# Layer 0 of a two-layer trunk: the kv latent normed ahead of its split, key copies and rotary digit products on ScalarE, and 8 instead of 16 diagonal convolution products on TensorE

## The chip, the core and the metric

The kernel is one program on one core of a Trainium2 chip. Five engines work beside each other, each through its own list of instructions in order: TensorE (PE; its weight loads are listed apart as PEld), VectorE (DVE), ScalarE (ACT), GpSimd (POOL) and SyncE (SP), which only issues transfers. The metric is device time in microseconds (us) of one execution; less is better.

## The reference

The input is 512 tokens of 1024 channels, in float32. Layer 0, which alone is touched, is a mixer in two branches followed by a gated MLP:

```python
proj = h @ w_in                          # h = rmsnorm(x)
# branch A: 512 channels
u = a * jax.nn.sigmoid(g)
u = causal_dwconv(u, conv_w, conv_b)     # 31 taps per channel
u = jax.nn.silu(layernorm(u, conv_ln_g, conv_ln_b))
# branch B: latent attention, 8 heads, causal, blocks of 128 queries
q  = rmsnorm(cq, q_norm_g) @ w_uq        # cq: 384 columns of proj
kv = rmsnorm(ckv, kv_norm_g) @ w_ukv     # ckv: 256 columns of proj
kn, v = kv[..., :64], kv[..., 64:]
# qr, kr are turned by cos, sin of position * inv_freq
o = mla_attention(qn, qr, kn, kr, v)
x = x + concat([u, o]) @ w_out
```

Layer 1 has a pooling mixer instead, and the same MLP. A last rmsnorm ends the trunk.

## The kernel before

Channels lie on the 128 partitions and the 512 tokens on the free axis, so that one projection of 128 columns is a sum of products 128x128 by 128x512 in a bank of PSUM. For float32 precision every operand is split in a high and a low part (`split`, lines 96 to 99: ACT copies the high part, DVE subtracts it from the source), and `mm3` (107 to 110) makes three products of the parts. Each weight tile of 128x1024 comes from memory through SP, and is split by the same two lines; three weight tiles can be held in parts at a time, so ACT can start on the next one only when TensorE has done with the oldest.

The order of each engine's instructions is set by a scheduler when the program is built, from the order of the code, buffers and dependencies; once built, it is fixed, and an engine whose next instruction waits does nothing else.

Layer 0 goes as follows.

- Start: x and the first weights arrive, xg = x times gain is split, and four banks are summed (356, 357). Meanwhile `rotary` (317 to 347) makes the tables of cosine and sine: an angle in two parts times five digits gives ten tiles `rope` of 128x64 (324, 325), which `fold` (313) reduces. The row sums of x*x go through small products on TensorE (`rstd`, 239), a reciprocal square root on DVE (205 to 212) and products with a diagonal on TensorE (`spread`, 260, 261), and ACT copies the result (265): a tile `rows` that holds the scale of each token on all partitions.
- Projections: `project` (364) makes one bank from 24 products. `latent` (448) makes three of cq and two of ckv: each is split from PSUM with its gain (102, 103), before its norm is known, and its squares are summed. After one more projection (kr) `rstd` gives the scales of q and kv together (465). Two pairs a and g of branch A follow.
- Attention (565 to 595): `keys_of` makes the keys of two heads and scales them on DVE by `rows_kv` (487), for which `spread` runs at the first call (483); the values are scaled by ACT (582). Each head has `scores` (product 511, DVE mask and maximum 514, ACT exponential 525, ACT scaling 532), `transposes` (546, ACT copies 548) and `values` (558).
- The convolution runs in the background. Channel tiles 0 to 2 are summed by DVE, one `tap` (400) for each of 30 shifts after an opening by ACT (383), in the PSUM tile `conv`. For tile 3 the first `PE_TAPS` = 16 shifts are products with a diagonal on TensorE (393; POOL makes the diagonal, 392), two in each of the eight heads, in the tile `aux`, and DVE does the other 15 there. `pump` (422) hands out these steps during the projections and heads; `pump(200, 200)` (595) hands out what is left behind the last head. `close` (415) copies the finished tile to `side`.
- End of the mixer: TensorE sums the attention half of the output projection (`half`), transposes the four `side` tiles (623), DVE takes mean and variance (625, 626), the reciprocal root and the scaling follow (634 to 637), TensorE transposes back (648), ACT applies silu (650), and the convolution half of the output projection follows (674 to 681), then the residual (663).

Of the kernel before, what the change touches and what calls it, by code (L numbers as in the profile page):

```python
# [8 lines left out]
F32 = mybir.dt.float32  # L9
F32R = mybir.dt.float32r  # L10
I32 = mybir.dt.int32
AF = mybir.ActivationFunctionType
ALU = mybir.AluOpType
# [11 lines left out]
SCALE = 1.0 / math.sqrt(96.0)  # L25
# [7 lines left out]
C_NE, C_CB, C_LG, C_LB, C_QG, C_KG, C_NO, C_PS, C_NF, C_FN = 0, 8, 12, 16, 20, 23, 25, 33, 41, 57  # L33
# [3 lines left out]
N_COL = C_FB + 2 * NF  # L37

WARM = 40
PE_TAPS = 16  # L40
PAD = 184
GLU, LAT, BLK, END = 3, 4, 2, 0

# [2 lines left out]
def kernel(  # L46
# [20 lines left out]
    act, dve, pool, pe = nc.scalar, nc.vector, nc.gpsimd, nc.tensor  # L67
# [21 lines left out]
    def temp():  # L89
        return p_t.tile([P, 2 + S], F32, tag="t", name=uid("t"))[:, :S]  # L90
# [5 lines left out]
    def split(dst, src):  # L96
        i = act.copy(dst[0], src)  # L97
        dve.tensor_tensor(dst[1], src, dst[0].bitcast(F32), op=ALU.subtract)  # L98
        return i
# [12 lines left out]
    def pair(t, lo=0, hi=S):  # L112
        if isinstance(t, tuple):
            return t[0][:, lo:hi], t[1][:, lo:hi]
        return t[:, 0, lo:hi], t[:, 1, lo:hi]
# [61 lines left out]
    spare, floor, q_scale = misc[:, 0:1], misc[:, 4:8], misc[:, 8:12]  # L177
# [3 lines left out]
    ps = bank()  # L181
# [7 lines left out]
    def c(i):  # L189
        return col[:, i : i + 1]  # L190
# [39 lines left out]
    def rstd(stats, blocks=range(4), floor=None, keep=None):  # L230

        ps = aux()
        nb = len(blocks)
        v = small(nb * len(stats))
        for k, st in enumerate(stats):
            for i, b in enumerate(blocks):
                at = 2 * (nb * k + i)
                for n, t in enumerate(st.parts):
                    pe.matmul(  # L239
                        ps[:, at : at + 2], t[:, b * P : (b + 1) * P], ones[:, 0:2],  # L240
                        start=n == 0, stop=n == len(st.parts) - 1,
                    )
            cols_of = ps[:, 2 * nb * k : 2 * nb * (k + 1) : 2]
            vk = v[:, nb * k : nb * (k + 1)]
            if floor is None:
                dve.tensor_scalar(vk, cols_of, 1.0 / st.n, EPS, op0=ALU.mult, op1=ALU.add)
            else:
                dve.scalar_tensor_tensor(
                    vk, cols_of, 1.0 / st.n, floor, op0=ALU.mult, op1=ALU.add
                )  # L250
        if keep is not None:
            dve.tensor_scalar(keep, v, EPS, None, op0=ALU.mult)
        return rsqrt(v, nb * len(stats))
# [10 lines left out]
    def spread(r, dst):  # L264
        act.copy(dst, spread_bank(r, 4))

    def rows_tile():
        return p_t.tile([P, S], F32, tag="rows", bufs=2, name=uid("rows"))
# [31 lines left out]
    ah = p_t.tile([P, 64], F32R, tag="rope_h", bufs=1, name="ah")  # L300
# [7 lines left out]
    ang, al, yt, yc, rr = (rt[:, i, :] for i in range(5))  # L308
# [8 lines left out]
    def rotary():  # L317
        dve.tensor_copy(yt, pos_i)
        dve.tensor_scalar(ang, yt, dig[:, 0:1], None, op0=ALU.mult)
        dve.tensor_copy(ah, ang)  # L320
        dve.tensor_tensor(al, ang, ah.bitcast(F32), op=ALU.subtract)
        for j in range(5):
            d = dig[:, 1 + j : 2 + j]
            dve.tensor_scalar(pr[:, 2 * j, :], ah.bitcast(F32), d, None, op0=ALU.mult)
            dve.tensor_scalar(pr[:, 2 * j + 1, :], al, d, None, op0=ALU.mult)
        fold(pr, rd, HUGE)
        fold(pr, rd, BIG)
        dve.tensor_reduce(yt, pr.rearrange("p j t -> p t j"), axis=AX.X, op=ALU.add)
        fold(yt, rr, BIG)
        dve.tensor_scalar(yc, yt, 0.25, None, op0=ALU.add)  # L330
        fold(yc, rr, BIG)
        for v in (yt, yc):
            dve.tensor_scalar(v, v, -TURN_LIMIT, TURN_LIMIT, op0=ALU.max, op1=ALU.min)
        for i, (v, s) in enumerate(((yc, 1.0), (yt, -1.0), (yt, 1.0))):
            act.activation(trig[:, i, :], v, AF.Sin, scale=s * 2.0 * math.pi)
        bounce = p_d.tile([64, S], F32, name="rope_rows")
        for g, i in enumerate((0, 0, 1, 2)):
            nc.sync.dma_start(
                bounce[g * 16 : (g + 1) * 16, :].rearrange("f (b t) -> (f b) t", b=8),
                trig[:, i, :],  # L340
            )
        pool.memset(ctab[0][0:64, :], 1.0)
        pool.memset(ctab[1][64:128, :], 1.0)
        nc.sync.dma_start(ctab[0][64:128, :], bounce)
        nc.sync.dma_start(ctab[1][0:64, :], bounce)
        nc.sync.dma_start(ktab[0:64, :], bounce)
        nc.sync.dma_start(ktab[64:128, :], bounce)
# [16 lines left out]
    def project():  # L364
        w = weights()
        ps = bank()
        for k in range(KD):
            mm3(ps, part(w, k), pair(xg[k]), k == 0, k == KD - 1)
        return ps
# [52 lines left out]
    def pump(nd, np_=0):  # L422
        for _ in range(min(np_, len(pe_work))):
            pe_work.pop(0)()
        for _ in range(min(nd, len(work))):
            work.pop(0)()
# [16 lines left out]
    def s4():  # L443
        return p_m.tile([P, 2, S], F32R, tag="s4", bufs=8, name=uid("s4"))
# [3 lines left out]
    def latent(n, gain, width):  # L448
        parts, stat = [], Squares(width, dve)
        for m in range(n):  # L450
            ps = project()
            parts.append(s4())
            split_scaled(pair(parts[m]), ps, c(gain + m))
            stat.add(ps)
            pump(LAT)
        return parts, stat

    cq, stat_q = latent(3, C_QG, 384)
    ckv, stat_kv = latent(2, C_KG, 256)

    ps = project()
    dve.tensor_tensor(ktab, ktab, rows0, op=ALU.mult)
    kt = temp()
    dve.tensor_tensor(kt, ps, ktab, op=ALU.mult)
    r = rstd([stat_q, stat_kv], floor=floor)
    r_q, r_kv = r[:, 0:4], r[:, 4:8]
    dve.tensor_scalar(q_scale, r_q, SCALE, None, op0=ALU.mult)
    for _ in range(2):
        ps_a = project()
        pump(GLU)  # L470
# [7 lines left out]
    def keys_of(hp):  # L478
        ps = bank()
        for k in range(2):  # L480
            mm3(ps, part(wk, k * 4 + hp), pair(ckv[k]), k == 0, k == 1)
        if hp == 0:
            spread(r_kv, rows_kv)
        ks = keys[hp % 2]
        for e in range(2):
            a, b = e * 64, e * 64 + 64
            dve.tensor_tensor(ks[a:b, e, :], ps[a:b, :], rows_kv[a:b, :], op=ALU.mult)

    qs, probs, pts, sums, att = {}, {}, {}, {}, []
    wq = [None]  # L490
# [71 lines left out]
        a = e * 64  # L562
        split(rows_of(att[hp], a, a + 64), ps[a : a + 64, :])

    rows_kv = rows_tile()
    queries(0)
    queries(1)
    ps = bank()
# [8 lines left out]
    for j in range(4):  # L577
        ps = bank()
        for k in range(2):
            mm3(ps, pair(ckv[k], j * P, (j + 1) * P), part(wv, k, S), k == 0, k == 1)  # L580
        v = p_a.tile([P, S], F32, tag="v", bufs=4, name=uid("v"))
        act.activation(v, ps, AF.Copy, scale=r_kv[:, j : j + 1])
        vals.append(v)
    for h in range(HEADS):
        scores(h)
# [415 lines left out]
```

## Time and profile before

| | us |
|---|---|
| median of 3 runs | 1013.87 |
| lowest, highest run | 1013.25, 1014.61 |
| the profiled execution's own time | 1013.5 |
| its span, first to last instruction | 1011.7 |
| TensorE busy | 994.0 (98%) |
| VectorE busy | 591.6 (58%) |
| ScalarE busy | 400.7 (40%) |
| GpSimd busy | 70.8 (7%) |

Busy times are those of the profiled execution, over its whole span. Layer 0's mixer takes the first 222 us or so of it; the remaining 790 us, in which the MLPs lie, are outside of the change. Times of day below count from the span's first instruction. A row of the profile gives a line of the kernel, the engine, the operation, what is written and what is read (numbers of buffers left out), and shapes. Consecutive instructions of an engine overlap, so a duration is a little longer than the step from one start to the next: a convolution tap on DVE lasts 0.74 to 0.75 us, and the next instruction starts 0.66 us after it if it doesn't need the tap's result.

### The profile page before, as it was taken

To read this page: it belongs to the slowest core of one execution; us is meant where nothing else is said; L and a number is where in the kernel's file an instruction comes from. 1 tells how busy PE (TensorE), PEld (TensorE's weight loads), DVE (VectorE), ACT (ScalarE), POOL (GpSimd) and SP (SyncE) were. 2 spreads that over 40 slices of the span, in tenths; PEclk is the share of its full clock that TensorE was granted. 3 is DMA by queue.
4 is the path that set the end of the run, shared out by engine and by line. 5 is a ranking of instruction groups with operands and counts; after the bars stand their busy time and mean duration, and the time that the engine had idled before them with its cause. 6 is when DMAs were issued, how large, how long until landed. Compare 5 with 4: busy or idle time off the path is not lost.

```text
span 1011.7 us, 11545 instructions
## 1 busy us (share of the span) xinstructions
PE 994.0 (98%) x4476; PEld 797.1 (79%) x4476; DVE 591.6 (58%) x915; ACT 400.7 (40%) x581; POOL 70.8 (7%) x107
## 2 busy tenths in 40 slices
PE   8999999999999999999999999999999999999996
PEld 6787676777888888888888889888888888888886
DVE  5889989856766565656332338485656555522223
ACT  6534687553433333333222236253333333332321
POOL 6000100012000000000001103100000000000101
PEclk9999999999999999999999999999999999999998
DMA  6422101113232323232222241322232223222212
GB/s 213 153 79 88 54 10 63 42 42 124 68 121 84 104 87 102 84 103 90 98 93 95 95 144 43 105 86 102 83 105 91 97 86 102 95 93 96 92 42 84
DMA packets 29478, 91.99 MB, mean 91 GB/s; under 512 B 4080, under 2 KB 6384, under 8 KB 29424
## 3 DMA queue, kind: packets, MB, share of 16 engines
q1 hardware_dynamic: 28880, 90.74, 27.3%
q8 instruction: 35, 0.57, 0.2%
q10 hardware_dynamic: 544, 0.52, 0.1%
q14 instruction: 19, 0.16, 0.0%
HBM read 89.02 MB, written 2.23 MB: 90 GB/s over the span
## 4 chain that ended last, share of the span: by engine, by line
PE 92%; DVE 4%; issue 1%; ACT 1%; DMA 0%; POOL 0%; SPq 0%; DVEq 0%
PE ps L108 28%; PE ps L110 28%; PE ps L109 28%; PE ps L558 2%; PE ps L511 1%; DVE lo L98 1%; PE aux L393 1%; PE ps L546 1%; PE aux L261 1%; PE aux L239 1%; DVE xgl L103 1%; DMA x<-in_xT_dram 0%; POOL sqr L226 0%; PE ps L869 0%; PE ps L870 0%
## 5 line engine op out<-in xcount | busy, mean ns | idle before, releaser
L108 PE MATMUL ps<-xgh,hi 128*128 128x512 f32 x816 | 324.0, 397 | 3.1 <-ACT hi L97 3.1
L97 ACT CAST hi<-raw 128x1024 fp32r<-128x1024 f32 (+2 forms) x166 | 170.0, 1026 | 394.2 <-PE ps L109 371.3
L110 PE MATMUL ps<-xgh,lo 128*128 128x512 f32 x816 | 323.3, 397 | 0.8 <-DVE lo L98 0.8
L109 PE MATMUL ps<-xgl,hi 128*128 128x512 f32 x816 | 323.4, 396 | 0.0
L98 DVE TENSOR_TENSOR lo<-raw,hi 128x1024 fp32r<-128x1024 f32 (+2 forms) x166 | 201.7, 1216 | 159.8 <-ACT hi L97 159.4
L108 PEld LDWEIGHTS ps<-xgh,hi 128*128 128x128 f32 x816 | 153.7, 188 | 40.2 <-ACT hi L97 3.7
L110 PEld LDWEIGHTS ps<-xgh,lo 128*128 128x128 f32 x816 | 153.8, 189 | 39.0 <-DVE lo L98 2.2
L109 PEld LDWEIGHTS ps<-xgl,hi 128*128 128x128 f32 x816 | 153.7, 188 | 36.6
L108 PE MATMUL ps<-gh,hi 128*128 128x512 f32 (+1 forms) x374 | 143.0, 382 | 0.0
L109 PE MATMUL ps<-gl,hi 128*128 128x512 f32 (+1 forms) x374 | 142.8, 382 | 0.0
L110 PE MATMUL ps<-gh,lo 128*128 128x512 f32 (+1 forms) x374 | 142.8, 382 | 0.0
L108 PEld LDWEIGHTS ps<-gh,hi 128*128 128x128 f32 x374 | 70.3, 188 | 15.0
L110 PEld LDWEIGHTS ps<-gh,lo 128*128 128x128 f32 x374 | 70.3, 188 | 15.0
L109 PEld LDWEIGHTS ps<-gl,hi 128*128 128x128 f32 x374 | 70.3, 188 | 15.0
L698 DVE TENSOR_TENSOR t<-ps,rows 128x512 f32<-128x512 f32 x44 | 30.4, 690 | 82.7 <-PE ps L110 82.7
L710 DVE TENSOR_TENSOR t<-ps,rows 128x512 f32<-128x512 f32 x44 | 30.4, 690 | 74.0 <-PE ps L110 74.0
L226 POOL TENSOR_TENSOR sqr<-sqr,sqr 128x512 f32<-128x512 f32 x33 | 50.5, 1529 | 322.2 <-ACT sqr L224 292.0
L400 DVE SCALAR_TENSOR_TENSOR conv<-u,col,conv 128x512 f32<-128x512 f32 x90 | 67.5, 750 | 1.6 <-ACT conv L383 0.7
L705 DVE SCALAR_TENSOR_TENSOR t<-t,col,t 128x512 f32<-128x512 f32 x88 | 65.6, 748 | 1.4
L708 ACT ACTIVATE t<-t 128x512 f32<-128x512 f32 x44 | 27.8, 632 | 74.2 <-DVE t L705 74.2
L103 DVE SCALAR_TENSOR_TENSOR xgl<-x,col,xgh 128x512 fp32r<-128x512 f32 x32 | 32.7, 1038 | 12.9 <-ACT xgh L102 12.9
L108 PE MATMUL ps<-s,hi 128*128 128x512 f32 x96 | 39.3, 421 | 0.0
(182 smaller groups left out, 813.6 us busy)
## 6 DMA issues: line engine op xcount, KB each, us to landing
raw<-in_w_up_dram SPq DMA_DIRECT2D x88, 512.0 KB, 3.3
raw<-in_w_down_dram SPq DMA_DIRECT2D x44, 512.0 KB, 3.3
raw<-in_w_in_dram SPq DMA_DIRECT2D x10, 512.0 KB, 3.3
raw<-in_w_out_dram SPq DMA_DIRECT2D x8, 512.0 KB, 3.3
x<-in_xT_dram SPq DMA_DIRECT2D x8, 256.0 KB, 4.7
raw<-in_w_in_dram SPq DMA_DIRECT2D x8, 256.0 KB, 4.0
raw<-in_w_uq_dram SPq DMA_DIRECT2D x4, 384.0 KB, 3.0
raw<-in_w_ukv_dram SPq DMA_DIRECT2D x2, 512.0 KB, 3.5
```

The costliest lines, as they stand in the source:

```text
L97: i = act.copy(dst[0], src)
L98: dve.tensor_tensor(dst[1], src, dst[0].bitcast(F32), op=ALU.subtract)
L103: dve.scalar_tensor_tensor(dst[1], src, scale, dst[0].bitcast(F32), op0=ALU.mult, op1=ALU.subtract)
L108: pe.matmul(ps, a[0], b[0], start=start, stop=False)
L109: pe.matmul(ps, a[0], b[1], start=False, stop=False)
L110: pe.matmul(ps, a[1], b[0], start=False, stop=stop)
L226: self.engine.tensor_tensor(self.parts[0], self.parts[0], t, op=ALU.add)
L400: i = dve.scalar_tensor_tensor(st["acc"], u[m][:, j : j + S], c(cw + j), st["acc"], op0=ALU.mult, op1=ALU.add,)
L698: dve.tensor_tensor(ut[:, 2 : 2 + S], pu, rows, op=ALU.mult)
L705: dve.scalar_tensor_tensor(a, ut[:, j : j + S], c(fw + j * NF + f), a, op0=ALU.mult, op1=ALU.add)
L708: act.activation(a, a, AF.Silu)
L710: dve.tensor_tensor(b, pv, rows, op=ALU.mult)
```

## The change

Four things change, all in layer 0.

1. `PE_TAPS` is 8. Tile 3 of the convolution has 8 products on TensorE in place of 16, and 23 taps on DVE in place of 15.
2. The ten products of the rotary digits are ACT's instead of DVE's.
3. The kv latent is normed before it is split. Its two banks stay in PSUM until their squares are summed, `rstd` and `spread` run for kv alone, and DVE multiplies each bank by gain and `rows_kv` into a temporary, which is then split. The two squares are kept apart, so `rstd` takes eight small products for kv in place of four. The norm of q has its own `rstd`, four products as before, and its own reciprocal root.
4. Keys and values need no scale any more: ACT copies the keys (eight copies of 64x512) in place of DVE's products, and copies the values without scale. The later `spread` falls away.

```diff
-PE_TAPS = 16
+PE_TAPS = 8
...
-            dve.tensor_scalar(pr[:, 2 * j, :], ah.bitcast(F32), d, None, op0=ALU.mult)
-            dve.tensor_scalar(pr[:, 2 * j + 1, :], al, d, None, op0=ALU.mult)
+            act.activation(pr[:, 2 * j, :], ah.bitcast(F32), AF.Copy, scale=d)
+            act.activation(pr[:, 2 * j + 1, :], al, AF.Copy, scale=d)
...
-    ckv, stat_kv = latent(2, C_KG, 256)
+
+    stat_kv, kv_ps, ckv = Squares(256, dve), [], []
+    for m in range(2):
+        kv_ps.append(project())
+        stat_kv.add(kv_ps[m], last=True)
+        pump(LAT)
+    rows_kv = rows_tile()
+    spread(rstd([stat_kv], floor=floor), rows_kv)
+    for m in range(2):
+        t = temp()
+        dve.scalar_tensor_tensor(
+            t, kv_ps[m], c(C_KG + m), rows_kv, op0=ALU.mult, op1=ALU.mult
+        )
+        ckv.append(s4())
+        split(pair(ckv[m]), t)
...
-    r = rstd([stat_q, stat_kv], floor=floor)
-    r_q, r_kv = r[:, 0:4], r[:, 4:8]
-    dve.tensor_scalar(q_scale, r_q, SCALE, None, op0=ALU.mult)
+    r = rstd([stat_q], floor=floor)
+    dve.tensor_scalar(q_scale, r, SCALE, None, op0=ALU.mult)
...
-        if hp == 0:
-            spread(r_kv, rows_kv)
...
-            dve.tensor_tensor(ks[a:b, e, :], ps[a:b, :], rows_kv[a:b, :], op=ALU.mult)
+            act.copy(ks[a:b, e, :], ps[a:b, :])
...
-        act.activation(v, ps, AF.Copy, scale=r_kv[:, j : j + 1])
+        act.copy(v, ps)
```

The scheduler then places the instructions anew. Three places matter below. Lines of the changed kernel stand about ten higher from the attention on: 522 is the score product 511, 635 the statistics 625.

TensorE, the scores of the fifth of the eight heads, before; `aux` is the sum of convolution tile 3, `tap` its diagonal:

```order
L511 MATMUL ps_1322<-keys_897,q_1229 128x128
L511 MATMUL ps_1327<-keys_897,q_1229 128x256
L393 MATMUL aux_1022<-u_884,tap_1333 128x512
L511 MATMUL ps_1338<-keys_897,q_1229 128x384
L511 MATMUL ps_1343<-keys_897,q_1229 128x512
L393 MATMUL aux_1022<-u_884,tap_1349 128x512
```

The same place now:

```order
L522 MATMUL ps_1345<-keys_935,q_1252 128x128
L522 MATMUL ps_1350<-keys_935,q_1252 128x256
L522 MATMUL ps_1358<-keys_935,q_1252 128x384
L522 MATMUL ps_1363<-keys_935,q_1252 128x512
L108 MATMUL ps_1376<-s_710,hi_939 128x512
```

Heads 1 to 4 keep their two diagonal products each, and heads 5 to 8 lose theirs.

VectorE, behind the kv projections, now; `d` are the diagonals of `spread`, line 469 is the new product with `rows`:

```order
L260 TENSOR_SCALAR d_695<-sq,s_681 128x128
L260 TENSOR_SCALAR d_698<-sq,s_681 128x128
L260 TENSOR_SCALAR d_701<-sq,s_681 128x128
L260 TENSOR_SCALAR d_704<-sq,s_681 128x128
L469 SCALAR_TENSOR_TENSOR t_708<-ps_600,col,rows_668 128x512
L469 SCALAR_TENSOR_TENSOR t_713<-ps_637,col,rows_668 128x512
L478 TENSOR_TENSOR t_750<-ps_724,ktab 128x512
```

Between the diagonals and the use of `rows`, which TensorE and ScalarE make from them, VectorE has nothing else to do; before, convolution taps stood between the diagonals, and `rows` was used by the keys some 25 instructions later.

VectorE, from the middle of the convolution's last taps to the statistics, before (behind the last head; `s` is the low part of the attention output):

```order
L530 RECIPROCAL s_1557<-s_1557 128x4
L98 TENSOR_TENSOR s_1546<-ps_1612,s_1546 64x512
L400 SCALAR_TENSOR_TENSOR aux_1022<-u_884,col,aux_1022 128x512
L98 TENSOR_TENSOR s_1632<-ps_1633,s_1632 64x512
L400 SCALAR_TENSOR_TENSOR aux_1022<-u_884,col,aux_1022 128x512 x11
L98 TENSOR_TENSOR s_1632<-ps_1750,s_1632 64x512
L625 BN_STATS bn_1715<-aux_1710 128x6
```

And now, from the second of the low parts `s` on:

```order
L98 TENSOR_TENSOR s_1639<-ps_1640,s_1639 64x512
L400 SCALAR_TENSOR_TENSOR aux_1045<-u_922,col,aux_1045 128x512
L98 TENSOR_TENSOR lo_1650<-raw_1647,hi_1649 128x1024
L400 SCALAR_TENSOR_TENSOR aux_1045<-u_922,col,aux_1045 128x512
L98 TENSOR_TENSOR lo_1694<-raw_1691,hi_1693 128x1024
L400 SCALAR_TENSOR_TENSOR aux_1045<-u_922,col,aux_1045 128x512 x4
L98 TENSOR_TENSOR s_1639<-ps_1757,s_1639 64x512
L400 SCALAR_TENSOR_TENSOR aux_1045<-u_922,col,aux_1045 128x512 x3
L98 TENSOR_TENSOR lo_1799<-raw_1796,hi_1798 128x1024
...
L98 TENSOR_TENSOR lo_1897<-raw_1894,hi_1896 128x1024
L400 SCALAR_TENSOR_TENSOR aux_1045<-u_922,col,aux_1045 128x512
L635 BN_STATS bn_1722<-aux_1717 128x6
```

Five low parts of weight tiles now stand among the last taps, of which before two stood in the heads and three behind the first statistics. In all, 17 taps stand behind the last score block of head 8 before, and 25 now; ahead of it there are 88 in both.

## Rows read from the trace of the kernel before

**Rows 1.** The page's first part: busy us, share of the span, instructions.
```profile
PE 994.0 (98%) x4476; PEld 797.1 (79%) x4476; DVE 591.6 (58%) x915; ACT 400.7 (40%) x581; POOL 70.8 (7%) x107
```
**Rows 2.** Stretches: start:end length, busy us per engine, PE's granted clock, DMA.
```profile
104.00:136.10 32.10, 32.10 (x132) 21.81 (x132) 30.58 (x75) 21.47 (x53) 5.00 (x8) 1.00 0.11 34
136.10:175.30 39.20, 39.13 (x168) 26.07 (x167) 36.10 (x87) 30.57 (x72) 2.93 (x5) 1.00 0.12 41
175.30:190.50 15.20, 15.20 (x72) 11.61 (x71) 13.80 (x21) 8.70 (x19) 0.00 (x0) 1.00 0.00 0
190.50:204.50 14.00, 12.13 (x63) 8.73 (x61) 10.98 (x29) 7.76 (x12) 0.10 (x1) 1.00 0.25 79
```
**Rows 3.** Timeline of PE, start: start us, duration, row, [idle before, releaser].
```profile
26.94 0.95 PE L239 MATMUL aux<-sq,sqr 128*128 128x2 f32 x8
...
36.14 0.91 PE L261 MATMUL aux<-d,sq 128*128 128x128 f32 x6 [1.63 <-DVE d L260]
...
38.05 0.38 PE L261 MATMUL aux<-d,sq 128*128 128x128 f32 x2
```
**Rows 4.** Timeline of DVE in the same stretch.
```profile
26.99 0.49 DVE L314 TENSOR_SCALAR rope<-rope 128x640 f32<-128x640 f32 x1
...
29.27 0.15 DVE L246 TENSOR_SCALAR s<-aux 128x4 f32<-128x4 f32 x1
...
35.71 0.68 DVE L260 TENSOR_SCALAR d<-sq,s 128x128 f32<-128x128 f32 x3
```
**Rows 5.** Timeline of ACT, the same stretch.
```profile
35.76 0.55 ACT L335 ACTIVATE t<-t 128x64 f32<-128x64 f32 x3
```
**Rows 6.** Timeline of PE, scores of head 8.
```profile
168.73 1.02 PE L393 MATMUL aux<-u,tap 128*128 128x512 f32 x2
169.59 0.81 PE L511 MATMUL ps<-keys,q 128*128 128x384 f32 x2
```
**Rows 7.** Groups of heads 5 to 8 (136.1 to 175.3): busy us, mean ns | idle before.
```profile
L400 DVE SCALAR_TENSOR_TENSOR conv<-u,col,conv 128x512 f32<-128x512 f32 x28 | 20.9, 746 | 0.6 <-ACT conv L383 0.5
...
L98 DVE TENSOR_TENSOR lo<-raw,hi 128x1024 fp32r<-128x1024 f32 x3 | 3.6, 1205 | 0.0
...
L487 DVE TENSOR_TENSOR keys<-ps,rows 64x512 f32<-64x512 f32 x2 | 1.4, 684 | 0.0
...
L530 DVE RECIPROCAL s<-s 128x4 f32<-128x4 f32 x4 | 0.7, 170 | 1.7 <-ACT prob L525 1.7
```
**Rows 8.** Timeline of DVE behind head 8.
```profile
175.22 0.74 DVE L400 SCALAR_TENSOR_TENSOR conv<-u,col,conv 128x512 f32<-128x512 f32 x1
175.88 0.14 DVE L521 SCALAR_TENSOR_TENSOR s<-s,misc 128x2 f32<-128x2 f32 x1
...
180.90 8.65 DVE L400 SCALAR_TENSOR_TENSOR aux<-u,col,aux 128x512 f32<-128x512 f32 x11
...
191.97 0.70 DVE L625 BATCH_NORM_STATS2 bn<-aux 128x6 f32<-128x512 f32 x1 [0.77 <-PE aux L623]
...
194.65 1.21 DVE L98 TENSOR_TENSOR lo<-raw,hi 128x1024 fp32r<-128x1024 f32 x1
195.77 0.17 DVE L626 BATCH_NORM_AGGREGATE misc<-bn 128x2 f32<-128x6 f32 x1
...
197.78 0.17 DVE L634 TENSOR_SCALAR s<-misc 128x4 f32<-128x4 f32 x1
```
**Rows 9.** Timeline of ACT, the close of convolution tile 3.
```profile
190.50 0.69 ACT L415 ACTIVATE side<-aux,col 128x512 f32<-128x512 f32 x1
```
**Rows 10.** Timeline of PE, the transposes back.
```profile
200.86 0.30 PE L648 MATMUL aux<-sq,t 128*128 128x128 f32 x1 [1.06 <-DVE t L637]
```
**Rows 11.** Stretches at the start, columns as in Rows 2.
```profile
14.00:17.00 3.00, 0.58 (x3) 0.26 (x2) 1.03 (x2) 2.69 (x5) 2.84 (x3) 1.00 0.85 285
...
18.00:19.00 1.00, 1.00 (x3) 0.81 (x3) 1.00 (x1) 0.45 (x1) 1.00 (x1) 0.50 0.28 16
...
21.00:22.00 1.00, 1.00 (x5) 0.79 (x5) 0.97 (x4) 0.00 (x0) 1.00 (x2) 0.96 0.05 12
```

More of the change, by code (lines that the diff above doesn't have):

```diff
@@ L563, in values @@
         split(rows_of(att[hp], a, a + 64), ps[a : a + 64, :])
-    rows_kv = rows_tile()
     queries(0)
```

## The prediction, made before the changed kernel ran

> **What bounds the kernel now.** I read the page's first part, then the stretches of the mixer with every engine's busy time, then the timelines of TensorE and VectorE where a stretch shows two engines near full. TensorE is busy for 98% of the span and VectorE for 58% [rows 1]. That average hides the stage that the change touches. In heads 1 to 4 TensorE is never idle, with VectorE at 30.58 of 32.10 us; in heads 5 to 8 TensorE has 39.13 and VectorE 36.10 of 39.20 us; behind the last head 15.20 and 13.80 of 15.20 us [rows 2]. Two engines have nearly the same work there, so what is taken from one and given to the other can't come out as the first one's gain. And the mixer's end is no longer TensorE's: from 190.5 on it has gaps, and the transposes back begin at 200.86 after 1.06 us of waiting for VectorE [rows 2, 10]. That instant is the one to follow: ahead of it TensorE has other work to fill in; behind it come the convolution half of the output projection and all the rest, which the change leaves alone. So the change is worth what it does to 200.86, plus what happens to TensorE's clock.
>
> **The start (products of digits).** TensorE reaches the products of `spread` early and waits 1.63 us for VectorE's diagonal, which starts at 35.71 [rows 3, 4]. Ten small products leave VectorE ahead of that. ACT makes one such 128x64 operation in about 0.18 us (three in 0.55, [rows 5]), so ten are 1.8 us, which fit in ACT's waits for weights. `fold`, now at 26.99, could then begin about 2.2 us earlier, but 29.27 takes the row sums, which TensorE delivers at 26.94 + 0.95 = 27.9 [rows 3, 4]. So VectorE is early by 29.3 - 27.9 = 1.4 us, and no more. Not all of it arrives: on ACT one weight cast now stands behind the first two sines, and the weight's low part on VectorE is ahead of the fourth diagonal. I put the fourth product, now at 38.05 [rows 3], 0.9 us earlier; bounds are 0 and the whole wait of 1.63.
>
> **The kv latent.** TensorE gets four small products more: 0.8 us by the four at 26.94 (0.95 with the overlap, [rows 3]). `spread` is moved, not added: its 0.9 us are paid earlier and saved before the first keys. VectorE gets a second reciprocal root, eleven instructions or some 2 us, and one wait: the product with `rows` stands right behind the diagonals, and TensorE and ACT must act in between. I estimate 2 to 3 us of idle VectorE. Queued behind it are the low parts of kv, q's root and the taps; nobody on TensorE needs these before the keys, 20 us later. By the order the taps are four behind here, but level (60) at the scores of head 4. So heads 1 to 4 start and end as now, but for -0.9 + 0.8 = -0.1 us: head 4's last score block is masked at 136.0 instead of 136.1. ACT's eight key copies replace VectorE's eight products (684 ns, [rows 7]), and ACT has 30.57 busy of 39.20 us [rows 2], so I cost them at nothing; were that cover gone, they would cost 0.6 us each time.
>
> **Heads 5 to 8.** TensorE loses eight diagonal products. One is worth 169.59 - 168.73 = 0.86 us [rows 6], so 6.9 in all, and TensorE needs 39.2 - 6.9 = 32.3 us. VectorE has 28 taps here before and after by the order and [rows 7]; it loses two of its three weight low parts (1.12 us each by the step 194.65 to 195.77, [rows 8]) and two key products (0.6 each): 36.1 - 3.5 = 32.6 us. Now VectorE is the longer one, if by a hair. Of its 3.1 us of idle time (39.20 - 36.10) 2.2 lie at one reciprocal and one opening [rows 7], which the new order puts behind taps; I leave 0.9. That gives 33.5 us and head 8's end at 169.5, 5.8 us earlier than 175.3. Bounds: 168.3 (TensorE paces) and 171.7 (all idle time stays).
>
> **Behind head 8.** This is where the taps land that TensorE no longer makes. Before, from 175.22 to 180.90 + 8.65 = 189.55, VectorE does 17 taps and two low parts `s` in 14.3 us [rows 8]. A tap costs 0.66 us beside other work (175.22 to 175.88) and 8.65/11 = 0.79 where it follows another one of the same tile [rows 8]. After, there are 25 taps, three `s`, and five weight low parts: 25 x 0.66 + 7 followers x 0.13 + 3 x 0.61 + 5 x 1.12 + 0.2 = 25.0 us, and 0.3 more, by which the same sum for before falls short of its 14.3. The last tap ends at 169.5 + 25.3 = 194.8, 5.3 us later than now. The fifth low part needs a weight buffer that TensorE frees only at the end of its attention sums; by my count TensorE gets there at 192 to 193, so this wait is 0 to 1 us; I take 0.2.
>
> From there some comes back. ACT closed the tile 0.95 us after the last tap (190.50, [rows 8, 9]), since a cast that waited for TensorE stood ahead; that one is early now: -0.75. From the first statistics to the root 191.97 to 197.78 passes, with two low parts of 1.12 us in it [rows 8], which are now ahead of the taps' end: -2.3. So 200.86 becomes 200.86 + 5.5 - 0.75 - 2.3 = 203.3, or 2.4 us later. Bounds: 1.2 less if TensorE paces the heads, 2.2 more if the idle time stays.
>
> **The clock.** TensorE ends its attention sums at 192 to 193 now, and has transposes alone until 203.3. After its wait of over 2 us at the start (0.58 busy of 3.00 us) the clock fell: the next three slices of 1 us from 18 to 21 were granted 0.50, the 1.2 GHz level, and 21 to 22 was at 0.96 [rows 11]. Half of the pace for 3 us is 1.5 us lost. The wait of 1.63 us at the start and the gaps around 200 left it at 1.00 [rows 2, 3]. The new gaps are of the kind that cost it, so I add 1.5; bounds 0 and 3 (a second fall). The Trainium skill, TensorE: Matmul & The Clock Gate, HAM oscillation — how this bites in real kernels, says the same against a kernel that empties its TensorE: a gap sends the array back to half rate, and the products after it pay. The trace agrees at 18 to 21; by this rule the added 1.5 is due, and without it the forecast would be 1015.9.
>
> **Sum.** 2.4 + 1.5 = 3.9 us on the profiled execution's own 1013.5 (span 1011.7) gives 1017.4. The median of the runs is 0.4 above that execution, which is inside their spread; I leave it out.
>
> **Rivals.**
> *TensorE stays the bound, and its lighter load arrives.* Then -6.9 + 0.8 - 0.9 = -7.0, or 1006.5; half-way, if the tail is filled better than I count, 1010. For it: 98% busy, and no idle time in heads 1 to 4. Against it: the busy shares of rows 2, and that the eight taps stand last, in the one chain that TensorE waits for already [rows 10]. The Trainium skill, Perfetto Trace Analysis, Identifying the Most-Contended Engine, says to find the engine with the highest occupancy and to optimize it first, and so speaks for this rival; the next section there speaks of kernels whose contended engine changes from stage to stage, and rows 2 show such a change.
> *A draw.* The heads pace by TensorE (-1.2), the start gives its whole 1.63 (-0.7), the clock holds: 2.4 - 1.9 = +0.5, or 1014. For it: each of the three is within its bounds. Against: all of them are needed.
> *Much slower.* The idle time in the heads stays (+2.2), TensorE, late by it, holds up the fifth low part (+1.0), and in the longer gap the clock falls twice (+1.5): 1017.4 + 4.7 = 1022. It decides from 2 us of waits in heads 5 to 8 on. ACT would be the place: 30.57 busy us against a stage shortened to 33.5 leaves it little.
> *The change doesn't do what it says:* TensorE's products do go, by the order; nothing more to ask.
>
> **Chances.** Slower as worked out, 1015.9 to 1020: 0.47; much slower: 0.11; draw, within 2 us: 0.20; TensorE's gain arrives, in part or whole: 0.22. About 0.2%, or 2 us, is what a measurement of this kernel tells from no change. The likeliest case alone spans 1015.5 to 1020; the range over the cases, 1010 to 1021, leaves out the full gain and the double fall.
>
> **What would show it.** Right: the wait at 36.14 nearly gone; no diagonal products in heads 5 to 8 and VectorE almost without idle time there; the last tap near 195; two waits of TensorE, of 2 us and more, ahead of the first transposes of `side` and ahead of the transposes back near 203; a granted clock of 0.5 for about 3 us right after; the stretch from there to the end as long as before, but for that. Wrong: the transposes back at 200 or earlier, or a full clock behind them.

## The result: 5.9 us slower, and the profile after

The changed kernel takes 1019.98 us (median of 6 runs, 1019.25 to 1021.49) against 1014.12 for the kernel before (6 runs): ratio 1.0062, 95% interval 1.0051 to 1.0072. The profiled execution of after is the longest of its runs, 1021.49 us (span 1019.6), 1.5 over their median; places in its trace are compared with each other and with those of before, not with the medians. In every cut below, behind attention a line number of after is 10 higher than that of before; runs of after with products by zeros add 2 to it behind the zeros, runs with low parts on GpSimd 4 from line 162 on.

The stretches of after, for those of [rows 2] and one more; the columns are busy us of PE, PEld, DVE, ACT and POOL, PE's granted clock, DMA share and GB/s:

```profile
104.00:136.10 32.10, 32.10 (x131) 21.98 (x130) 29.73 (x71) 23.14 (x55) 3.09 (x4) 1.00 0.14 47
136.10:175.30 39.20, 38.01 (x171) 25.87 (x170) 37.49 (x93) 35.53 (x86) 0.00 (x0) 1.00 0.04 14
175.30:190.50 15.20, 15.20 (x72) 12.02 (x71) 14.13 (x20) 6.99 (x12) 0.00 (x0) 1.00 0.21 69
190.50:204.50 14.00, 7.46 (x31) 5.51 (x29) 10.39 (x21) 4.43 (x7) 0.00 (x0) 0.77 0.36 112
204.50:222.00 17.50, 14.51 (x55) 11.53 (x56) 5.80 (x16) 4.84 (x8) 0.10 (x1) 0.69 0.00 1
```

Up to 190.5 TensorE is nearly as busy as it was: 1.2 us are missing in the second stretch (38.01 of 39.20), 0.9 of them one wait for ScalarE. From there to 204.5 it works 7.46 us where it worked 12.13, and the clock, at 1.00 before, is at 0.77 and then 0.69. What it waits for stands in its timeline (start, duration, row, idle time before and its releaser):

```profile
198.20 1.12 PE L633 MATMUL aux<-sq,side 128*128 128x128 f32 x4 [3.54 <-ACT side L415]
...
200.73 1.12 PE L633 MATMUL aux<-sq,side 128*128 128x128 f32 x4 [1.20 <-ACT t L638]
...
206.84 0.44 PE L658 MATMUL aux<-sq,t 128*128 128x128 f32 x1 [4.14 <-DVE t L647]
```

The last row answers to [rows 10]: 206.84 for 200.86, with 4.14 us of waiting for 1.06. VectorE's timeline of the same stretch, for [rows 8]:

```profile
170.29 0.75 DVE L400 SCALAR_TENSOR_TENSOR conv<-u,col,conv 128x512 f32<-128x512 f32 x1
...
186.90 0.69 DVE L98 TENSOR_TENSOR s<-ps,s 64x512 fp32r<-64x512 f32 x1 [0.80 <-ACT s L97]
...
190.00 1.23 DVE L98 TENSOR_TENSOR lo<-raw,hi 128x1024 fp32r<-128x1024 f32 x1
191.14 0.75 DVE L400 SCALAR_TENSOR_TENSOR aux<-u,col,aux 128x512 f32<-128x512 f32 x1
191.80 1.22 DVE L98 TENSOR_TENSOR lo<-raw,hi 128x1024 fp32r<-128x1024 f32 x1
...
195.54 1.22 DVE L98 TENSOR_TENSOR lo<-raw,hi 128x1024 fp32r<-128x1024 f32 x1 [0.27 <-ACT hi L97]
196.68 0.75 DVE L400 SCALAR_TENSOR_TENSOR aux<-u,col,aux 128x512 f32<-128x512 f32 x1
199.36 0.70 DVE L635 BATCH_NORM_STATS2 bn<-aux 128x6 f32<-128x512 f32 x1 [1.93 <-PE aux L633]
...
203.69 0.17 DVE L644 TENSOR_SCALAR s<-misc 128x4 f32<-128x4 f32 x1
```

Head 8's last score block is done at 170.29, 5 us earlier than before; the last tap ends at 196.68 + 0.75 = 197.43, 7.9 us later. Weight low parts (`lo`) stand among the taps; in [rows 8] the one at 194.65 stands behind them. Where all this ends is the first addition to the residual. Before (a row not shown so far):

```profile
218.12 2.09 DVE L663 TENSOR_TENSOR x<-ps,x 128x512 f32<-128x512 f32 x3 [9.96 <-PE ps L110]
```

and after:

```profile
226.53 2.09 DVE L673 TENSOR_TENSOR x<-ps,x 128x512 f32<-128x512 f32 x3 [12.25 <-PE ps L110]
```

The rest of the span is 1011.7 - 218.12 = 793.6 us before and 1019.6 - 226.53 = 793.1 after: next to nothing is lost or won behind it. So it serves as the mark for the experiments; where a run has another such rest, it is said. As runs differ by up to 1.7 us in when the first weights arrive, marks are also counted from the fourth product of the start.

### The profile page after: what moved, and what is told of

Read it like the earlier page. It is cut to its first block, busy times and chain, and to the rows that moved or that the text cites. A ratio compares the mean times of both kernels' runs of the same rounds, so it can differ in the third digit from the quotient of the medians.

```text
span 1019.6 us, 11550 instructions
## 1 busy us (share of the span) xinstructions
PE 994.8 (98%) x4468; PEld 798.0 (78%) x4468; DVE 591.9 (58%) x917; ACT 406.0 (40%) x599; POOL 65.8 (6%) x99
## 4 chain that ended last, share of the span: by engine, by line
PE 92%; DVE 5%; DMA 1%; ACT 1%; issue 1%; SPq 0%; DVEq 0%; ACTq 0%
PE ps L108 28%; PE ps L109 28%; PE ps L110 28%; PE ps L569 1%; DVE lo L98 1%; PE ps L522 1%; PE ps L557 1%; PE aux L393 1%; PE aux L239 1%; DVE xgl L103 1%; PE aux L261 1%; DMA x<-in_xT_dram 1%; DVE conv L400 0%; DMA raw<-in_w_in_dram 0%; DMA col<-in_cols_dram 0%
```

## Experiments

Each kernel ran in turn with the kernel before; ratios are to that.

### The changed kernel with 16 products

```diff
-PE_TAPS = 8
+PE_TAPS = 16
```

> The changed kernel with 16 diagonal products on TensorE as before; the kv norm ahead of the split, ScalarE's key copies and ScalarE's rotary products stay. Theory (the eight taps and the weight low parts behind head 8 delay the statistics of the convolution, and TensorE's clock falls in the waits): 17 taps and no weight low part stand behind head 8 again, the transposes back begin at 199 to 201, the clock stays at 1.00 there, and the time is 1012 to 1014.5. Rival (the new wait of VectorE at the kv norm, or ScalarE's heavier load in the heads, makes it slow): the time stays at 1018 or more.

Measured: 1012.57 us, ratio 0.9989 [0.998, 0.9998]. In PE's timeline the transposes back are where they were:

```profile
200.00 0.30 PE L658 MATMUL aux<-sq,t 128*128 128x128 f32 x1 [0.84 <-DVE t L647]
```

The clock is 1.00 from 190.5 to 222. So the whole loss hangs on the eight products; the other parts together are a gain at the edge of what can be told.

### The kernel before with 8 products

```diff
-PE_TAPS = 16
+PE_TAPS = 8
```

> The kernel before with 8 diagonal products and nothing else changed. Theory: VectorE has eight taps more and keeps its key products, so its last tap ends at 196 to 199, TensorE waits, the clock falls, and the time is 1020 to 1024. Rival 1 (TensorE is the bound): 1007 to 1010. Rival 2 (the kv norm or ScalarE's load is to blame): 1013 to 1015.

Measured: 1020.55 us, ratio 1.0070 [1.0057, 1.0083]. PE's timeline shows the same waits with nothing else changed:

```profile
198.40 0.66 PE L623 MATMUL aux<-sq,side 128*128 128x128 f32 x4 [4.34 <-ACT side L415]
...
206.57 0.45 PE L648 MATMUL aux<-sq,t 128*128 128x128 f32 x1 [4.14 <-DVE t L637]
```

Alone the eight products cost what the whole change costs.

### Twelve and twenty products

```diff
-PE_TAPS = 8
+PE_TAPS = 12        # and 20 in the second
```

> The changed kernel with 12 of the masks' diagonal products on TensorE instead of 8. Theory (VectorE's row of taps behind head 8 sets the end, and the clock falls because TensorE then stands waiting): four taps of 0.66 us leave the tail, so the last tap ends 2.6 us earlier, near 194.8, and the transposes back start near 203.5 (206.84 with 8, 200.00 with 16); TensorE still waits over 2 us there, so the clock falls as with 8 and its cost stays. Time about 1016.5 (1015 to 1018), half way or a little more between 1012.6 (16 products) and 1020.0 (8). Rival 1 (the loss is a step that comes with the fall of the clock alone): about 1019 or over. Rival 2 (TensorE bounds heads 5 to 8, so that fewer products are a gain as long as the tail is not late): at or below 1012.6.

Measured: 1017.08 us, ratio 1.0034 [1.0022, 1.0047], as the theory had it. The transposes back start at 202.58 (near 203.5 expected) behind a wait of 5.13 us, and the clock is at 0.50 from 202 to 204.

> The changed kernel with 20 products on TensorE. With 16, TensorE waits only 0.84 us before the transposes back, so the VectorE tail cannot give back more than that. Theory (with 16 the two engines are level, and beyond it TensorE is the bound in heads 5 to 8): four products of 0.86 us add 3.4 us to TensorE, the shorter tail gives back up to 0.84; time 1015 to 1016 (2.5 to 3.5 over 1012.6), transposes back near 202.5 to 203. Rival (VectorE bounds the whole stretch, TensorE has room): 1012 or less.

Measured: 1012.82 us, ratio 0.9993 [0.9985, 1.0002]: neither. Against 16 products four more cost 0.25 us (0.4 by the ratios), which the intervals, some 0.9 us wide to either side, don't tell from nothing; 2.5 to 3.5 were expected. The stretches (columns as above) show TensorE without a gap:

```profile
136.10:175.30 39.20, 39.20 (x160) 25.46 (x160) 36.75 (x85) 30.07 (x70) 4.83 (x8) 1.00 0.12 41
...
190.50:204.50 14.00, 14.00 (x73) 11.10 (x72) 11.30 (x29) 9.43 (x14) 0.10 (x1) 1.00 0.24 76
```

My error was to count only the 0.84 us of waiting ahead of the transposes as room. With 16 products TensorE's attention sums end at 198.78 + 0.23 = 199.0 and the output products begin at 203.66: 4.65 us for 16 transposes, which with nothing in their way take 16 x 0.11 = 1.8. So 2.9 us of room, against 4 x 0.86 = 3.4 us of work. A tap costs TensorE 0.86 us in the heads or VectorE 0.66 behind them; from 16 to 20 that trade is even, as far as these runs can tell.

### Products by zeros in TensorE's waits

```diff
+    half(2, att, range(4), True, w2)
+    for n, zero_by in ((5, causal), (5, ys[3])):   # (12, ys[3]) in the second
+        for _ in range(n):
+            pe.matmul(accs[4][:, :384], causal[:, :P], zero_by[:, :384],
+                      start=False, stop=False)
     for m in range(4):
-        if m % 2 == 0:
-            half(2, att, (m, m + 1), True, w2)
```

> The changed kernel with ten products of zeros (f32, 128x384) added to a sum of the output projection: five behind the attention sums, five around the second transposes of side. They add nothing to the result and only keep TensorE at work in its two long waits; VectorE's order is the same. Theory: the granted clock stays at 1.00 from 194 to 216, the transposes and the first products behind 206 run at full pace, the waits stay: 2 to 4 us less than the changed kernel, 1016 to 1018. Rival (the lower clock is a sign, not a cost): 1020 to 1022.

Measured: 1018.99 us, ratio 1.0050 [1.0038, 1.0063]: only 1 us less, a miss. The products left a wait open, and the transposes behind it ran at half rate all the same (0.45 for 0.30 us; granted clock 0.50 from 206 to 210):

```profile
205.54 0.45 PE L660 MATMUL aux<-sq,t 128*128 128x128 f32 x1 [3.00 <-DVE t L647]
```

> The changed kernel with products by a block of zeros in the two waits of TensorE behind head 8: 5 before the first transposes as in the earlier such run, and 12 instead of 5 behind the last of them, enough for the 3.0 us that were left open there. Nothing that VectorE does is changed, so the transposes back start as before, at 205 to 206.5. Theory (part of the loss is the clock, which falls to half because TensorE stands): the granted clock stays at 1.00 from 190 to 222, the eight first transposes back take 0.23 us apart or less, and the first addition to the residual comes near 222.5 to 223.5 (226.53 with the change alone, 224.20 with the fewer zero products); time 1016.5 to 1017.8. Then the tail alone is worth about 4.5 us and the clock about 3. Rival (the fall is no cost, or comes whatever TensorE does there): 1019 to 1020 and a clock of 0.8 or less in 204.5 to 222.

Measured: 1017.71 us, ratio 1.0040 [1.0026, 1.0054]. The timeline of PE and the stretches:

```profile
201.09 5.97 PE L656 MATMUL ps<-side,causal 128*128 128x384 f32 x18
206.89 0.60 PE L660 MATMUL aux<-sq,t 128*128 128x128 f32 x4
```

```profile
190.50:204.50 14.00, 13.68 (x56) 9.14 (x55) 10.84 (x27) 4.07 (x6) 0.00 (x0) 1.00 0.34 114
204.50:222.00 17.50, 17.05 (x77) 12.99 (x77) 4.73 (x10) 4.85 (x8) 0.10 (x1) 1.00 0.00 0
```

VectorE's timeline, the first addition:

```profile
223.14 2.09 DVE L675 TENSOR_TENSOR x<-ps,x 128x512 f32<-128x512 f32 x3 [9.95 <-PE ps L110]
```

The clock stays at 1.00, and the time falls by 1019.98 - 1017.71 = 2.3 us (0.22% by the ratios, give or take 0.17). VectorE's order is that of the changed kernel, and the attention products that the edit draws together ended ahead of the first wait there too. So by the medians the clock costs 2.3 us, give or take 1.7. The price is rather higher, as the zeros hold up the work themselves: the second transposes of `side` start 1.84 us behind the first statistics (198.37 to 200.21; before 1.37, 191.97 to 193.34), and the transposes back at 206.89, 1.3 us later than with fewer zeros; 1.0 of that comes back, as they then run in one go (223.14 - 206.89 = 16.25 to the first addition, 17.26 before). That is 0.8 us in all. By my estimate from these rows the clock is worth some 3 us, and of the 1017.71 - 1012.57 = 5.1 us that are left some 4.3 are VectorE's tail at full clock.

The Trainium skill, TensorE: Matmul & The Clock Gate, HAM oscillation — how this bites in real kernels, says that matmuls behind a gap start at half rate; the trace agrees here: the same transposes at 0.50 behind a wait of 3.00 us, and at 1.00 behind products by zeros. It isn't so behind every gap: in the kernel before with 8 products the four transposes behind 4.34 us of waiting take 0.66 us, at full rate, and the clock falls only then (1.00 from 198 to 199, 0.51 from 199 to 200).

### Weight low parts on GpSimd

```diff
-        copied = split((hi, lo), raws[i])
+        if 24 <= i < 32:                       # 25 <= i < 29 in the second
+            copied = act.copy(hi, raws[i])
+            pool.tensor_tensor(lo, raws[i], hi.bitcast(F32), op=ALU.subtract)
+        else:
+            copied = split((hi, lo), raws[i])
```

> The changed kernel with the low parts of the eight output projection weight tiles made by GpSimd instead of VectorE, so that behind head 8 VectorE has its 25 taps but not the five weight low parts. Theory: the last tap ends 5 to 6 us earlier (191 to 192), the transposes back begin at 200 to 202, and the time is 1013 to 1016; less of it arrives if GpSimd's low parts (estimate 3 us each, from its 1.5 us for 128x512) slow VectorE or hold up the output projection. Rival (only the number of taps counts, since the low parts fill VectorE's waits): 1019 to 1020.

Measured: 1020.94 us, ratio 1.0072 [1.0060, 1.0085]: a miss. The tail did shorten (the last tap ended at 189.6) and the first addition came at 220.30, but two things took it back. Inside the root chain (the reciprocal root behind the statistics, from 197.78 on in [rows 8]) a 128x4 operation of VectorE, elsewhere 0.16 us, took 2.35; VectorE's and GpSimd's timelines:

```profile
197.35 2.35 DVE L215 SCALAR_TENSOR_TENSOR s<-s,s 128x4 f32<-128x4 f32 x1
```

```profile
197.34 2.34 POOL L162 TENSOR_TENSOR lo<-raw,hi 128x1024 fp32r<-128x1024 f32 x1 [2.68 <-ACT hi L161]
```

And the later tiles and the squares queued on GpSimd, so that TensorE waited for a low part; this is the run whose rest behind the mark is longer, 1019.1 - 220.30 = 798.8 us:

```profile
235.66 1.22 PE L110 MATMUL ps<-s,lo 128*128 128x512 f32 x2 [3.03 <-POOL lo L162]
```

> The changed kernel with the low parts of four weight tiles (those that VectorE computes among the taps behind head 8) on GpSimd; the ones after them go back to VectorE, as GpSimd held up TensorE by 3.0 us and the squares there in the earlier run. Theory (the tail's length sets the end): four times 1.14 us leave the tail, the last tap ends near 192.9, the root chain is not held up by GpSimd (one 128x4 operation of it took 2.35 us beside a GpSimd subtraction in the earlier run), the transposes back start near 202, the first addition to the residual at 218.5 to 221.5, depending on the clock; time 1013.5 to 1016. Rival (the tail is not what costs; GpSimd's work beside VectorE costs as much as it takes off): 1019 to 1021 as with all eight tiles moved.

Measured: 1014.44 us, ratio 1.0008 [0.9999, 1.0016], still with 8 products. VectorE's last taps, and TensorE:

```profile
186.46 3.92 DVE L404 SCALAR_TENSOR_TENSOR aux<-u,col,aux 128x512 f32<-128x512 f32 x5
```

```profile
200.45 0.44 PE L662 MATMUL aux<-sq,t 128*128 128x128 f32 x1 [4.33 <-DVE t L651]
```

The last tap ends at 186.46 + 3.92 = 190.4 and the transposes back start 6.4 us earlier than after, 5.2 counted from the start's fourth product. Four low parts of 1.14 us (by the step 190.00 to 191.14) are 4.6; the fifth, still VectorE's, moved out of the tail, behind the first statistics (195.24). So it is the length of VectorE's tail that sets the end, and the low parts in it weigh as much as the taps. (The clock still fell here, to 0.83 in 190.5 to 204.5.)

### The other parts by themselves

```diff
-            dve.tensor_scalar(pr[:, 2 * j, :], ah.bitcast(F32), d, None, op0=ALU.mult)
-            dve.tensor_scalar(pr[:, 2 * j + 1, :], al, d, None, op0=ALU.mult)
+            act.activation(pr[:, 2 * j, :], ah.bitcast(F32), AF.Copy, scale=d)
+            act.activation(pr[:, 2 * j + 1, :], al, AF.Copy, scale=d)
```

> The kernel before with the ten rotary digit products on ScalarE and nothing else changed. Theory (the start is the whole of the small gain that 16 products left over, 1.3 us): the fourth of the products by the scaled identity comes 9.8 to 10.2 us after the first product of the statistic, as in the runs of the changed kernel (11.1 before), TensorE's wait of 1.6 us there is 0.3 to 0.6, and all that follows comes earlier by as much; time 1.0 to 1.4 under that of before, near 1012.6. Rival (the gain came from the kv latent and the key copies, and the start's is given back behind it): no change against before.

Measured: 1012.16 us, ratio 0.9988 [0.9980, 0.9997], the lowest median here. PE's timeline, for [rows 3]: the wait is 0.26 for 1.63, the fourth product 36.62 - 26.86 = 9.76 us behind the statistic's (11.11 before).

```profile
26.86 0.95 PE L239 MATMUL aux<-sq,sqr 128*128 128x2 f32 x8
...
34.70 0.91 PE L261 MATMUL aux<-d,sq 128*128 128x128 f32 x6 [0.26 <-DVE d L260]
...
36.62 0.38 PE L261 MATMUL aux<-d,sq 128*128 128x128 f32 x2
```

The next kernel is the kv and key part of the change alone; against the changed kernel:

```diff
-PE_TAPS = 8
+PE_TAPS = 16
...
-            act.activation(pr[:, 2 * j, :], ah.bitcast(F32), AF.Copy, scale=d)
-            act.activation(pr[:, 2 * j + 1, :], al, AF.Copy, scale=d)
+            dve.tensor_scalar(pr[:, 2 * j, :], ah.bitcast(F32), d, None, op0=ALU.mult)
+            dve.tensor_scalar(pr[:, 2 * j + 1, :], al, d, None, op0=ALU.mult)
```

> The kernel before with the kv latent normed ahead of its split and the key copies on ScalarE, without the other two parts: 16 products, rotary digits on VectorE. Theory (this part moves work that lies beside other work; four more products of the statistic's form on TensorE, 0.2 to 0.8 us, against 8 fewer VectorE operations of 0.69 us between heads, which TensorE hides): within 0.4 us of before. Rival 1 (its wait of VectorE for the row of factors is paid): 1 to 3 us slower. Rival 2 (it is the gain that 16 products left over): 1.0 to 1.4 us faster.

Measured: 1014.82 us, ratio 1.0011 [1.0002, 1.0020], 1.3 us slower: more than I allowed, at the low end of rival 1's range, but not for its reason, as TensorE is busy without a gap from 37 to 137. From the fourth product of the start (38.08 here) to the transposes back it takes 201.88 - 38.08 = 163.8 us, 1.0 more than before (200.86 - 38.05 = 162.8), about the price of four more products of the statistic's form:

```profile
201.88 0.30 PE L658 MATMUL aux<-sq,t 128*128 128x128 f32 x1 [0.83 <-DVE t L647]
```

In the profiled run, the longest of its eleven (1015.65), another 1.0 us goes behind them, where the clock dipped (204 to 206):

```profile
204.00:206.00 2.00, 1.64 (x9) 1.65 (x9) 0.73 (x2) 2.00 (x5) 0.10 (x1) 0.50 0.37 109
```

With 16 products and all parts it did not dip in the run that was traced. The two parts' medians add up to 0 (-1.4 and +1.3), the kernel with both and 16 products had -1.3; the intervals, some 1 us wide to either side, allow both.

### Twelve products and four tiles on GpSimd

```diff
-PE_TAPS = 8
+PE_TAPS = 12        # and 25 <= i < 29 on GpSimd, as above
```

> The changed kernel with 12 products on TensorE and the low parts of the four weight tiles of the tail on GpSimd. Theory (time is set by the later of two rows behind head 8: TensorE's, which 4 products fewer shorten by 3.4 us against the kernel with 16, and VectorE's, which the four tiles shorten by 4.6 against the kernel with 12): the transposes back start near 198 (202.58 with 12 products alone), TensorE waits before them 0 to 2 us, the clock stays at full; time 1010 to 1012.5, under that of both kernels. Rival (GpSimd's subtractions hold up VectorE or TensorE as much as they relieve it, or TensorE is the bound at any number of products): 1013 to 1016.

Measured: 1013.51 us, ratio 1.0000 [0.9991, 1.0009]: a miss; it falls into the rival's range, but not for the rival's reasons. VectorE and TensorE:

```profile
171.80 0.68 DVE L529 CUSTOM_DVE_ANT_0 prob<-ps,causal 128x512 f32<-128x512 f32 x1
...
189.75 1.54 DVE L404 SCALAR_TENSOR_TENSOR aux<-u,col,aux 128x512 f32<-128x512 f32 x2
```

```profile
200.32 0.30 PE L662 MATMUL aux<-sq,t 128*128 128x128 f32 x1 [1.79 <-DVE t L651]
```

The last block of head 8 is masked at 171.80 where with 8 products and the same four tiles it was at 168.51 (2.5 later counted from the fourth product), and the last tap ends at 191.3 for 190.4, the same by that count. What four taps fewer take from the tail, four products more add to the heads. I had added up the two gains as if they lay in different stretches. No row here waits for GpSimd. And the clock didn't stay at full: it is at 0.76 from 200 to 205. The eleven executions part by their mean clock: five at 0.996 took 1011.92 to 1013.01 us, six at 0.992 to 0.994 took 1013.51 to 1014.72, and the traced one (1014.12) is of the six. So four of the five with the higher clock lie in the forecast's range; one program, with one order, can come out either way, and no trace here shows what decides it.

## Why the prediction was right, and where its sizes were off

It named the sign, the place and the mechanism: the eight taps stand last, in a row of VectorE for which TensorE waits already, and the clock falls in the wait. 8 products in the kernel before (1020.55) and 16 in the one after (1012.57) show that nothing else carries the loss. By size it fell short: 1017.4 forecast, 1019.98 measured, and 1021.49 in the profiled execution, whose places stand below. The places of the profiled runs, by the prediction's own steps:

| place | before | forecast | after |
|---|---|---|---|
| fourth product of the start | 38.05 | 37.15 | 37.33 |
| head 4's last score block done | 136.06 | 136.0 | 136.72 |
| head 8's last score block done | 175.2 | 169.5 | 170.29 |
| last tap ends | 189.55 | 194.8 | 197.43 |
| tile closed by ACT | 190.50 | 195.0 | 197.46 |
| root chain begins | 197.78 | 200.0 | 203.69 |
| transposes back | 200.86 | 203.3 | 206.84 |
| first addition to the residual | 218.12 | 222.1 | 226.53 |

(195.0 is 194.8 plus the 0.95 - 0.75 left of the close; 200.0 is 7.28 - 2.3 later; 222.1 is 203.3 + 17.26, the distance before, + 1.5. The sum for 203.3 counts the 0.2 for the fifth low part twice, in the 25.3 and in the 5.5: by its own terms it is 203.1.)

*The start.* TensorE's wait, 1.63 in [rows 3], is 0.57; its timeline in after:

```profile
27.27 0.95 PE L239 MATMUL aux<-sq,sqr 128*128 128x2 f32 x8
...
35.41 0.91 PE L261 MATMUL aux<-d,sq 128*128 128x128 f32 x6 [0.57 <-DVE d L260]
...
37.33 0.38 PE L261 MATMUL aux<-d,sq 128*128 128x128 f32 x2
```

Counted from the statistic the gain is 11.11 - 10.06 = 1.05 us (forecast 0.9), and the rotary digits alone give 1.4 in the median. Right; the place is 0.2 late, as the statistic itself came 0.3 later.

*The kv latent and the key copies*: a first term that was too small. The end of head 4 on VectorE (the read of the last block's maximum), before and after:

```profile
136.06 0.08 DVE L514 DVE_READ_ACCUMULATOR2_ANT s<- 128x1 f32 x1
```

```profile
136.72 0.07 DVE L525 DVE_READ_ACCUMULATOR2_ANT s<- 128x1 f32 x1
```

From the fourth product it takes 136.06 - 38.05 = 98.0 us before and 136.72 - 37.33 = 99.4 after: 1.4 more where I had 0.8, and head 4 ends 0.7 later where I had 0.1 earlier. The four products of the statistic's form alone make 1.0 (TensorE is busy with that form for 2.9 us there, 1.9 before); the other 0.4 I can't place, and with 16 products 1.0 is left at the transposes back. The idle VectorE is hidden as said: TensorE has no gap in that stretch.

*Heads 5 to 8.* From 136.72 to 170.29 it takes 33.57 us, forecast 33.5: right in sum, with luck in its terms. VectorE is busy for 32.06 of it (forecast 32.6) and waits for 1.5 (0.9), TensorE is busy for 32.38 (32.3). VectorE is the longer engine only at the end; until 163 it is TensorE that has next to no gap:

```profile
136.72:163.00 26.28, 26.12 (x118) 18.15 (x117) 24.77 (x61) 23.25 (x54) 0.00 (x0) 1.00 0.06 21
163.00:170.29 7.29, 6.26 (x28) 3.73 (x27) 7.29 (x21) 7.02 (x19) 0.00 (x0) 1.00 0.01 2
```

The groups of 136.1 to 175.3, columns as in [rows 7], show 28 + 6 taps, six of them behind head 8's last block. Of VectorE's 2.2 us of waits at a reciprocal and an opening nothing is left; what it waits for now is TensorE's score blocks (0.9) and casts (0.7):

```profile
L400 DVE SCALAR_TENSOR_TENSOR conv<-u,col,conv 128x512 f32<-128x512 f32 x28 | 20.9, 747 | 0.1
L400 DVE SCALAR_TENSOR_TENSOR aux<-u,col,aux 128x512 f32<-128x512 f32 x6 | 4.5, 748 | 0.0
...
L98 DVE TENSOR_TENSOR lo<-raw,hi 128x1024 fp32r<-128x1024 f32 x1 | 1.2, 1226 | 0.2 <-ACT hi L97 0.2
```

*Behind head 8*: the second, and the largest. 25.3 us counted, 197.43 - 170.29 = 27.1 taken. VectorE waits 0.80 + 0.27 + 0.17 = 1.2 us for casts of ACT where I had 0.2 for the fifth low part alone: the third `s` waits 0.80 for a cast that waits for TensorE. The 25 taps take 17.9 us for 17.4, as in a row of one tile's taps the last one keeps the longer step too (three in 2.37 us, 187.63 to 190.00), and the three `s` take 2.1 for 1.8. The 0.3 that the sum was given for falling short before was itself too little: 17 x 0.66 + 10 x 0.13 + 2 x 0.61 = 13.7 falls 0.6 short of 14.3. That the low parts stand in the tail was counted right, and the four tiles on GpSimd confirm their price.

*From the close to the root*: the third. 7.28 - 2.3 = 5.0 forecast, 203.69 - 197.46 = 6.2 taken. I had taken the low parts off and left the transposes their old pace, but the clock falls with the first of them: four take 1.12 us, where the first four in the kernel before with 8 products still take 0.66. It is the clock's price ahead of the transposes back, and I had put it behind them only: with the clock kept up by zeros the same way takes 5.5 us, 0.5 of which is the zeros' own.

*The clock*: the fourth. From the transposes back to the residual 226.53 - 206.84 = 19.69 us pass, 2.4 more than 17.26; forecast 1.5. The stretches of after show how long it stays down:

```profile
198.00:200.00 2.00, 1.33 (x5) 0.93 (x5) 0.64 (x2) 0.15 (x1) 0.00 (x0) 0.54 0.62 227
200.00:205.00 5.00, 1.97 (x8) 1.57 (x8) 3.59 (x15) 2.34 (x4) 0.00 (x0) 0.50 0.00 0
205.00:210.00 5.00, 2.51 (x11) 1.74 (x12) 2.78 (x10) 1.38 (x3) 0.00 (x0) 0.50 0.02 3
210.00:215.00 5.00, 5.00 (x16) 4.20 (x15) 2.59 (x4) 3.47 (x7) 0.10 (x1) 0.50 0.00 0
215.00:216.00 1.00, 1.00 (x5) 0.80 (x4) 0.00 (x0) 0.00 (x0) 0.00 (x0) 0.89 0.00 0
```

Some 17 us at 1.2 GHz, where I had taken the 3 us of [rows 11]. There TensorE worked without a gap once it had its weights; here transposes with waits between them follow, and the level is still 0.50 from 210 to 215, where it works again without a gap. So the fall costs 1.2 us ahead of the transposes back and 2.4 behind them in this execution, where I had 1.5 in all; by the zero products it is some 3. It isn't more, as most of those 17 us are waiting.

So the misses add up to 0.8 (start 0.2, kv 0.6, heads 5 to 8 under 0.1), 1.8 (tail), 1.2 (close to root) and 0.9 (clock behind). That makes 4.7 of the 4.4 between 222.1 and 226.53; the other 0.3 are differences of the opposite sign, the 0.2 counted twice and the close at once after the last tap.

*The rivals.* TensorE's lighter load did arrive, as 5.6 us in heads 5 to 8 (39.16 from the end of head 4 to that of head 8 before, 33.57 after), and was given back behind them; 98% of the span's busy time said nothing of that. That engine was relieved of 6.9 us, and the runs got 5.9 longer. *Much slower* at 1022 was off by its mechanism: of VectorE's idle time in the heads 1.5 us were left, less than the 2 it needed, and the fifth low part was held up by 0.27.

Left open: why the clock dipped in the traced execution of the kernel with the kv part alone and not in that of the kernel with all parts and 16 products, where the waits (0.83 or 0.84, and 0.76 us) are the same; the executions of either have mean clocks from 0.993 to 0.997, so it may come and go with the execution, but only one of each was traced; and a version clearly under both kernels. The rotary digits alone (1012.16) have the lowest median, 1.4 us under before.

## What to carry to other kernels

When work is moved between two engines, write down for each stretch which one is waited for at its end; a share over the span can't show it. Work moved onto an engine comes out in the row that others wait for, together with everything that used to stand behind that row in its queue: here five weight low parts weighed as much as the taps. And where a wait of TensorE opens, price the clock on both sides of it, for as long as its work stays scattered.

## What the runs showed of the hardware that I had not expected

A VectorE operation of 128x4 elements took 2.35 us, for exactly as long as a GpSimd subtraction (2.34 us) that had begun 0.01 us earlier; both read two operands from SBUF. Taps, which read one of theirs from PSUM, ran beside such subtractions at their usual 0.74 us (one at 157.65 in the same run, beside a subtraction that began at 157.25). The Trainium skill, SBUF — State Buffer, SBUF: two separate sides, says that the two engines share a pair of ports that one of them holds for a whole instruction, and names VectorE operations with two SBUF inputs; these rows agree.

ScalarE's product of 128x64 by a scale from SBUF takes 0.33 us and steps by 0.24, where I had estimated 0.18 from another form [rows 5]; ten are 2.4 us:

```profile
24.06 0.33 ACT L324 ACTIVATE rope<-ah,dig 128x64 f32<-128x64 f32 x1
24.30 0.33 ACT L325 ACTIVATE rope<-t,dig 128x64 f32<-128x64 f32 x1
```

GpSimd needs 2.3 to 2.8 us for a low part of 128x1024 that VectorE makes in 1.22.
